# The turn from the in- to the out-projection of the convolution layer: gate tiles taken piece by piece, one weight buffer fewer, four tiles normalised

## The chip, the cores and the metric

One core of one Trainium2 chip runs the whole program. The metric is device time in microseconds (us) of one execution; before the change it was 1757.4 us, the median of three (1753.49 to 1759.08). The engines are PE (TensorE, the matmuls), DVE (VectorE), ACT (ScalarE), POOL (GpSimd) and SP (SyncE, which here only issues DMAs, in the order in which they stand in its queue).

## The reference

Two layers on 2064 tokens (16 meta tokens and 2048 of the input), 1024 channels. The change lies inside the first layer, between its first and its last matrix product:

```python
def conformer_mixer(h, w_in, b_in, w_dw, b_dw, norm_g, norm_b, w_out, b_out):
    u = h @ w_in + b_in                                  # 1024 -> 3072
    a, ga, z = jnp.split(u, 3, axis=-1)
    glu = a * jax.nn.sigmoid(ga)
    c = causal depthwise convolution of glu, 31 taps, + b_dw
    c = jax.nn.silu(layer_norm(c, norm_g, norm_b))
    return (c * jax.nn.silu(z)) @ w_out + b_out          # 1024 -> 1024
...
h = layer_norm(sqrt(2) * h + y, post_ln_g[0], post_ln_b[0])
```

The second layer is a gated linear attention on the same stream; its code is not touched.

## The kernel before, in words

**Numbers.** Each float32 operand of a large product is split into a high and a low part (`split`: ACT copies the high part, L73; DVE or POOL subtracts it, L74). A product is three matmuls for each of 8 blocks of 128 rows: high by high (L106), high by low (L107), low by high (L108). So one result tile takes 24 matmuls.

**Phase 1, the in-projection.** The tokens lie in five pieces of 414 or 412 (`XCS`), and the output channels in tiles of 128: g, a and z, eight of each. g and a make the gated value, whose 31 taps run on ACT and POOL (products and sums) and on DVE (L204). A z tile goes through silu on ACT (L258) and out to DRAM (`sz_d`), and the convolved channels to `c_d`. Weights of a tile are loaded one tile ahead (`load_w`) into one of two pairs of buffers (`pair`). The last two z tiles, 6 and 7, are special: each does piece 0 first; then `right.close()` gives memory back and `hook()` opens phase 2 (`head`, in `body`); then z6 does its other four pieces, then z7 its own.

**Phase 2, the out-projection, tile by tile of 128 tokens (17 tiles, the last of 16).** `norm(i)` loads the convolved channels of tile i into one of `CB` = 4 buffers c (L316), sums over channels (DVE L321 for even i, a tree of three POOL additions for odd i, L341 to L343), gets the mean by a small matmul (L323), subtracts it (DVE L324), squares (ACT L325), adds up (POOL tree), and by two more small matmuls (L330, L335) has the scale in PSUM, by which DVE multiplies (L336). `gate(i)` applies silu (ACT L351, 8 instructions), multiplies by z (DVE L354, the z from `szb`, L349) and splits into h_gt and l_gt (ACT L73, DVE L74). `out_proj(i)` does two halves of 24 matmuls, pj_y, adds the residual (DVE L377) and the bias (POOL L423), and normalises: L385 to L388, ACT L396, DVE L397, POOL L398, then the store to `h1_d`.

**The weights of the out-projection** come in 8 blocks of 128 rows (`load_out_w`, L364): the raw block lands in one of the two `raw` buffers (blocks 0 and 1) or in a buffer of `wrp` (`wr`; blocks 2 to 7), of which there are `WRB` = 3. ACT makes woh of it, and POOL (blocks 0, 3, 6) or DVE (the rest) makes wol. A raw buffer is free when wol has been made.

**What sets the order.** The program is recorded in the order of the Python code, with every wait on a tile that is still in use, and a scheduler then sets the order of the instructions on each engine. On the chip each engine runs its list in that order: an instruction that waits holds up those behind it. c_i+4 takes the buffer of c_i, which is free after l_gt_i.

Of the kernel before, what the change touches and what calls it, by code (L numbers as in the profile page):

```python
# [12 lines left out]
F32R = mybir.dt.float32r  # L13
# [6 lines left out]
P = 128  # L20
D = 1024
KD = D // P
# [4 lines left out]
NXC = len(XCS)  # L27
# [5 lines left out]
ZSPL = 2  # L33
# [6 lines left out]
GRATE = 2.35  # L40
VCOST = 0.53
CB = 4
WRB = 3
WMAX = 1088
SUBS = [(P * i, P) for i in range(16)] + [(2048, 16)]
BLOCKS = ((0, 528), (528, 512), (1040, 512), (1552, 512))
# [3 lines left out]
class Trunk:  # L50
# [64 lines left out]
    def phase1(self, x_cm, w1, pp, c_d, sz_d, hook):  # L115
# [22 lines left out]
        x = {}  # L138
# [26 lines left out]
        def load_w(i):  # L165
            return self.load([w1[i]], f"w{i}", nc.gpsimd)
# [46 lines left out]
        def weave(na=22 / 15, nd=20 / 15, nd1=None):  # L213
            debt[0] += na
            while debt[0] >= 1:
                debt[0] -= 1
                if act_q:
                    act_q.popleft()()
            for s in range(2):
                debt[1 + s] += nd1 if s and nd1 is not None else nd  # L220
            while max(debt[1:]) >= 1:
                for s in range(2):
                    if debt[1 + s] >= 1:
                        debt[1 + s] -= 1
                        if dve_q[s] and dve_q[s][0][0]["done"]:
                            dve_q[s].popleft()[1]()
# [3 lines left out]
        def do_g(j, w, cs=range(NXC)):  # L230
            if 0 in cs:
                glus[j] = gup[j % 3].tile([P, HIST + T], F32, tag="glu", name=f"glu{j}")
                nc.any.memset(glus[j][:, 0:HIST], 0.0)
            for c in cs:
                pg = proj(w, c, f"g{j}")
                t0, n = XCS[c]
                nc.scalar.activation(
                    glus[j][:, HIST + t0 : HIST + t0 + n], pg, AF.Sigmoid, bias=b_in[:, 8 + j : 9 + j]
                )
                weave()  # L240

        def do_a(j, w, cs=range(NXC)):
            glu = glus[j]
            for c in cs:
                pa = proj(w, c, f"a{j}")
                t0, n = XCS[c]
                dst = glu[:, HIST + t0 : HIST + t0 + n]
                nc.vector.scalar_tensor_tensor(dst, pa, b_in[:, j : j + 1], dst, op0=ALU.add, op1=ALU.mult)
                weave()
                if c in (2, NXC - 1):  # L250
                    conv_ops(j, c // 3, glu)

        def do_z(j, w, cs=range(NXC)):
            for c in cs:
# [4 lines left out]
                nc.sync.dma_start(sz_d[:, j, t0 : t0 + n], sz)  # L259
                weave()  # L260

        for c in range(NXC):
            do_g(0, w0["g"], [c])
            do_a(0, w0["a"], [c])
        order = []
# [5 lines left out]

        split = len(order) + ZSPL
        order += [(do_z, j, 16 + j, [0]) for j in range(KD - ZSPL, KD)]
        order += [(do_z, j, 16 + j, range(1, NXC)) for j in range(KD - ZSPL, KD)]
        nxt = load_w(order[0][2])
        for i, (f, j, _, *cs) in enumerate(order):
            w, nxt = nxt, load_w(order[i + 1][2]) if i + 1 < len(order) else None
# [12 lines left out]
    def phase2_open(self, pp, c_d, sz_d):  # L290
# [5 lines left out]
        self.st2w = ExitStack()  # L296
        self.wrp = self.pool(self.st2w, name="p2r", bufs=WRB, side="right")
        self.prm2 = self.lp.tile([P, 16], F32, name="prm2", bufs=1)
# [46 lines left out]
    def gate(self, i, c):  # L345
        nc = self.nc
        t0, n = SUBS[i]
        sz = self.lp.tile([P, KD, P], F32, tag="szb", name=f"szb{i}")[:, :, :n]
        nc.sync.dma_start(sz, self.sz_d[:, :, t0 : t0 + n])  # L349
        for j in range(KD):  # L350
            nc.scalar.activation(  # L351
                c[:, j], c[:, j], AF.Silu, bias=self.prm2[:, 8 + j : 9 + j], scale=self.prm2[:, j : j + 1]
            )
        nc.vector.tensor_tensor(c, c, sz, op=ALU.mult)  # L354
        h, l = (t[:, :D].rearrange("p (k n) -> p k n", n=P)[:, :, :n] for t in self.pair(f"gt{i}"))
        self.split(c, h, l, nc.vector)
        return i, h, l

# [522 lines left out]
def body(tc, x_cm, x_tok, w1, pp1, wo1, pp2, rows, w2, wv0, wv, wa2, pp3, wo2, out):  # L881
    with ExitStack() as ctx:
        dram = ctx.enter_context(tc.tile_pool(name="dram", bufs=1, space=DRAM))
        c_d = dram.tile([P, KD, T], F32, name="c_d")
        sz_d = dram.tile([P, KD, T], F32, name="sz_d")
        h1_d = dram.tile([T, D], F32, name="h1_d")
        og_d = dram.tile([P, KD, T - NMETA], F32, name="og_d")
        t = Trunk(tc, ctx)
        t.h1_d = h1_d

        def head():
            t.phase2_open(pp2, c_d, sz_d)
            for _ in range(CB - 1):
                t.norm_next()
            t.gate_next()

        t.phase1(x_cm, w1, pp1, c_d, sz_d, head)
        t.phase2(x_tok, wo1, rows[0:3], h1_d, partial(t.phase3_open, (w2, wv0, wv)))
        t.phase3_init(wa2, pp3, og_d)
        t.phase4(wo2, rows[3:5], out)  # L900
# [52 lines left out]
```

## Time and profile before

| | us |
|---|---|
| time, median of 3 (lowest, highest) | 1757.4 (1753.49, 1759.08) |
| the profiled execution | 1755.36 |
| its span, first to last instruction | 1753.6 |
| PE busy in the span | 1702.3 (97%) |
| DVE, POOL, ACT busy | 1402.4 (80%), 944.3 (54%), 842.9 (48%) |
| last z matmul to the end of the out-projection | about 555 to 785 |

The span is PE's: of the 1753.6 us some 51 are not covered by a matmul, spread over many short waits. A time in a row is counted from the span's start. In a timeline the number behind the start is the duration, xN says that N instructions are merged, and [n <-X] says that the engine was idle for n us before and what ended that. PE's rows overlap, since matmuls are pipelined: what counts is the distance from start to start.

### The profile page before, as it was taken

The numbers are of one execution on the slowest core, as the hardware profiler recorded it, in microseconds if no ns is written. First come the engines' busy times: TensorE is split into PE (matmuls) and PEld (weight loads), VectorE is DVE, ScalarE is ACT, GpSimd is POOL, SyncE is SP. The second block draws the span as 40 slices with busy tenths as digits, with TensorE's granted clock in tenths as the row PEclk, the third lists the DMA queues.
The fourth block names the chain that finished last, engine by engine and source line by source line (L and its number), as shares of the span: only waits on it lengthen the run. The fifth ranks groups of instructions, "written<-read, shape, count | busy, mean of one in ns | idle before, by whom it ended". The sixth has DMA issues, their size and how long they took to land.

```text
span 1753.6 us, 29029 instructions
## 1 busy us (share of the span) xinstructions
PE 1702.3 (97%) x11715; PEld 1514.2 (86%) x11715; DVE 1402.4 (80%) x1869; ACT 842.9 (48%) x1269; POOL 944.3 (54%) x675
## 2 busy tenths in 40 slices
PE   8999999999998998999999999999999999999998
PEld 8999999999998776767888888888888878888886
DVE  5789999999998898777666687777878687887665
ACT  6445555655544454445455455555555455541000
POOL 0879999999975788756233233333333153331000
PEclk9999999999999999999999999999999999999999
DMA  7111111111256544433113222232223322354441
GB/s 244 37 37 37 37 69 40 73 56 54 75 169 217 173 162 139 140 124 99 67 61 109 87 92 78 84 105 79 85 85 96 111 73 85 123 165 162 147 135 62
DMA packets 103910, 178.72 MB, mean 102 GB/s; under 512 B 8624, under 2 KB 68400, under 8 KB 103776
## 3 DMA queue, kind: packets, MB, share of 16 engines
q1 hardware_dynamic: 103776, 176.86, 30.0%
q8 instruction: 92, 1.51, 0.4%
q14 instruction: 42, 0.34, 0.1%
HBM read 134.70 MB, written 42.14 MB: 101 GB/s over the span
## 4 chain that ended last, share of the span: by engine, by line
PE 72%; DVE 14%; POOL 5%; ACT 4%; issue 3%; DMA 2%; SPq 0%; DVEq 0%; POOLq 0%; ACTq 0%
PE pj_y L108 4%; PE pj_y L107 4%; PE pj_y L106 4%; PE pj_g L107 3%; PE pj_g L108 3%; PE pj_g L106 3%; PE pj_z L107 3%; PE pj_a L107 3%; PE pj_z L106 3%; PE pj_a L106 3%; PE pj_z L108 3%; PE pj_a L108 3%; PE sm L755 2%; DVE A L721 1%; DVE A L720 1%
## 5 line engine op out<-in xcount | busy, mean ns | idle before, releaser
L196 POOL TENSOR_TENSOR gacc<-gacc,prod 128x1024 f32<-128x1024 f32 (+1 forms) x156 | 385.9, 2477 | 65.2 <-ACT prod L195 56.2
L204 DVE SCALAR_TENSOR_TENSOR cacc<-glu,prm,cacc 128x1024 f32<-128x1024 f32 (+1 forms) x292 | 374.9, 1294 | 7.0
L717 POOL TENSOR_TENSOR A<-b 128x256 f32<-128x256 f32 x96 | 83.2, 867 | 292.1 <-DVE b L643 110.0
L195 ACT ACTIVATE prod<-glu,prm 128x1024 f32<-128x1024 f32 (+1 forms) x156 | 179.2, 1155 | 111.0 <-POOL gacc L196 110.8
L106 PE MATMUL pj_g<-xh,h_w 128*128 128x412 f32 (+1 forms) x320 | 114.2, 357 | 6.0 <-ACT h_w L73 4.2
L107 PE MATMUL pj_g<-xl,h_w 128*128 128x412 f32 (+1 forms) x320 | 114.0, 356 | 0.3 <-DVE xl L74 0.3
L108 PE MATMUL pj_y<-woh,l_gt 128*128 128x512 f32 (+1 forms) x272 | 108.3, 403 | 5.8 <-DVE l_gt L74 5.7
L108 PE MATMUL pj_g<-xh,l_w 128*128 128x412 f32 (+1 forms) x320 | 113.0, 354 | 0.0
L107 PE MATMUL pj_a<-xl,h_w 128*128 128x412 f32 (+1 forms) x320 | 112.4, 351 | 0.0
L106 PE MATMUL pj_a<-xh,h_w 128*128 128x412 f32 (+1 forms) x320 | 112.3, 351 | 0.0
L107 PE MATMUL pj_z<-xl,h_w 128*128 128x412 f32 (+1 forms) x320 | 112.3, 351 | 0.0
L106 PE MATMUL pj_z<-xh,h_w 128*128 128x412 f32 (+1 forms) x320 | 112.2, 351 | 0.0
L108 PE MATMUL pj_z<-xh,l_w 128*128 128x412 f32 (+1 forms) x320 | 112.0, 351 | 0.0
L108 PE MATMUL pj_a<-xh,l_w 128*128 128x412 f32 (+1 forms) x320 | 111.9, 350 | 0.0
L106 PE MATMUL pj_y<-woh,h_gt 128*128 128x512 f32 (+1 forms) x272 | 110.0, 407 | 1.3 <-ACT h_gt L73 1.2
L107 PE MATMUL pj_y<-wol,h_gt 128*128 128x512 f32 (+1 forms) x272 | 109.6, 403 | 0.0
L106 PE MATMUL pj_y<-w4h,h_g 128*128 128x512 f32 x256 | 99.6, 390 | 0.0
L108 PE MATMUL pj_y<-w4h,l_g 128*128 128x512 f32 x256 | 99.6, 390 | 0.0
L107 PE MATMUL pj_y<-w4l,h_g 128*128 128x512 f32 x256 | 99.6, 390 | 0.0
L654 ACT ACTIVATE A<-A 128x512 f32<-128x512 f32 (+1 forms) x112 | 66.7, 596 | 57.7 <-POOL A L718 56.4
L388 POOL TENSOR_TENSOR rs<-rs,mhalf 128x1 f32<-128x1 f32 x16 | 14.5, 905 | 145.8 <-DVE rs L387 145.8
L377 DVE SCALAR_TENSOR_TENSOR xt<-xt,pj_y 128x512 f32<-128x512 f32 (+1 forms) x66 | 44.5, 678 | 59.5 <-PE pj_y L108 59.4
(428 smaller groups left out, 5366.5 us busy)
## 6 DMA issues: line engine op xcount, KB each, us to landing
r_w<-w SPq DMA_DIRECT2D x24, 512.0 KB, 3.3
c<-c_d SPq DMA_DIRECT2D x16, 512.0 KB, 4.5
szb<-sz_d SPq DMA_DIRECT2D x16, 512.0 KB, 4.6
xt<-x_tok SPq DMA_DIRECT2D x16, 512.0 KB, 4.6
h_d<-xt SPq DMA_DIRECT2D x16, 512.0 KB, 2.8
r_h1b<-h_d SPq DMA_DIRECT2D x16, 512.0 KB, 3.9
og_d<-og SPq DMA_DIRECT2D x32, 256.0 KB, 3.4
xt<-h_d SPq DMA_DIRECT2D x16, 512.0 KB, 3.5
```

Of the source, the lines that this page charges most:

```text
L106: mm(out, lhsT=lh, rhs=rh, start=(i == 0), stop=False)
L107: mm(out, lhsT=lh, rhs=rl, start=False, stop=False)
L108: mm(out, lhsT=ll, rhs=rh, start=False, stop=(i == n - 1))
L195: nc.scalar.activation(pr, src(k), AF.Copy, scale=tap(k))
L196: nc.gpsimd.tensor_tensor(st["g"], st["g"], pr, op=ALU.add)
L204: nc.vector.scalar_tensor_tensor(out, src(k), tap(k), acc, op0=ALU.mult, op1=ALU.add)
L377: self.nc.vector.scalar_tensor_tensor(xt[:m, es], xt[:m, es], ALPHA, ps, op0=ALU.mult, op1=ALU.add)
L654: ex = lambda o, i: nc.scalar.activation(o, i, AF.Exp, scale=1.0 / TAU)
L717: nc.gpsimd.tensor_tensor(Av[:, :, 0], mid, bv[:, :, 0], op=ALU.subtract)
L720: nc.vector.tensor_tensor(Av[:, :, 0], Av[:, :, 0], kv[:, :, 0], op=ALU.mult)
L721: nc.vector.tensor_tensor(Av[:, :, 1], Av[:, :, 1], qv[:, :, 1], op=ALU.mult)
L755: nc.tensor.matmul(sm[s : s + 32, c, 48 + 32 * i : 80 + 32 * i], lhsT=lv[m][:, w], rhs=lv[m][:, w], start=True, stop=True, skip_group_chec ...
```

## The change

Four edits. The other pieces of z6 and z7 are no longer done tile after tile but piece by piece: piece 1 of z6, piece 1 of z7, piece 2 of z6, and so on (`do_zs`), so both weight tiles stay in use to the end. The gate of tile 0 has two buffers of its own (`gt0h`, `gt0l`), since neither of the two shared pairs is free then. The raw buffers of the out-projection's weights go from three to two (`WRB`). At the opening of phase 2 four tiles are normalised instead of three.

```diff
--- before.py
+++ after.py
@@ -40,7 +40,7 @@
 GRATE = 2.35
 VCOST = 0.53
 CB = 4
-WRB = 3
+WRB = 2
 WMAX = 1088
 SUBS = [(P * i, P) for i in range(16)] + [(2048, 16)]
 BLOCKS = ((0, 528), (528, 512), (1040, 512), (1552, 512))
@@ -259,6 +259,12 @@
                 nc.sync.dma_start(sz_d[:, j, t0 : t0 + n], sz)
                 weave()
 
+        def do_zs(js, w, cs):
+            ws = [w] + [load_w(16 + j) for j in js[1:]]
+            for c in cs:
+                for j, wj in zip(js, ws):
+                    do_z(j, wj, [c])
+
         for c in range(NXC):
             do_g(0, w0["g"], [c])
             do_a(0, w0["a"], [c])
@@ -271,7 +277,8 @@
 
         split = len(order) + ZSPL
         order += [(do_z, j, 16 + j, [0]) for j in range(KD - ZSPL, KD)]
-        order += [(do_z, j, 16 + j, range(1, NXC)) for j in range(KD - ZSPL, KD)]
+
+        order.append((do_zs, range(KD - ZSPL, KD), 16 + KD - ZSPL, range(1, NXC)))
         nxt = load_w(order[0][2])
         for i, (f, j, _, *cs) in enumerate(order):
             w, nxt = nxt, load_w(order[i + 1][2]) if i + 1 < len(order) else None
@@ -352,7 +359,9 @@
                 c[:, j], c[:, j], AF.Silu, bias=self.prm2[:, 8 + j : 9 + j], scale=self.prm2[:, j : j + 1]
             )
         nc.vector.tensor_tensor(c, c, sz, op=ALU.mult)
-        h, l = (t[:, :D].rearrange("p (k n) -> p k n", n=P)[:, :, :n] for t in self.pair(f"gt{i}"))
+
+        own = [self.lp.tile([P, D], F32R, name=f"gt0{x}", bufs=1) for x in "hl"] if i == 0 else self.pair(f"gt{i}")
+        h, l = (t[:, :D].rearrange("p (k n) -> p k n", n=P)[:, :, :n] for t in own)
         self.split(c, h, l, nc.vector)
         return i, h, l
 
@@ -890,7 +899,7 @@
 
         def head():
             t.phase2_open(pp2, c_d, sz_d)
-            for _ in range(CB - 1):
+            for _ in range(CB):
                 t.norm_next()
             t.gate_next()
 
```

The scheduler makes a new order of it from the piece after the turn up to the first blocks of the second layer; before and behind that the engines' lists are the same.

On PE, where the first two tiles of the out-projection (y0 with both halves, y1 with its first) stand beside each other; woh and wol are the weights' parts, the number behind them the block, gt the gated tile. Before, the rows that reach block 4:

```order
L107 MATMUL pj_y0_0_4687<-wol3_4614,h_gt0_4310 128x512
L108 MATMUL pj_y0_0_4687<-woh3_4613,l_gt0_4311 128x512
L106 MATMUL pj_y0_0_4687<-woh4_4619,h_gt0_4310 128x512
L107 MATMUL pj_y0_1_4713<-wol3_4614,h_gt0_4310 128x512
L108 MATMUL pj_y0_1_4713<-woh3_4613,l_gt0_4311 128x512
L106 MATMUL pj_y0_1_4713<-woh4_4619,h_gt0_4310 128x512
L107 MATMUL pj_y0_0_4687<-wol4_4620,h_gt0_4310 128x512
L108 MATMUL pj_y0_0_4687<-woh4_4619,l_gt0_4311 128x512
L107 MATMUL pj_y0_1_4713<-wol4_4620,h_gt0_4310 128x512
L108 MATMUL pj_y0_1_4713<-woh4_4619,l_gt0_4311 128x512
```

And with the change:

```order
L106 MATMUL pj_y1_0_4811<-woh3_4635,h_gt1_4701 128x512
L107 MATMUL pj_y1_0_4811<-wol3_4636,h_gt1_4701 128x512
L108 MATMUL pj_y1_0_4811<-woh3_4635,l_gt1_4702 128x512
L337 MATMUL rb3_4306<-mean_80,sq3_4295 128x1
L106 MATMUL pj_y0_0_4707<-woh4_4641,gt0h_4326 128x512
L106 MATMUL pj_y0_1_4733<-woh4_4641,gt0h_4326 128x512
L106 MATMUL pj_y1_0_4811<-woh4_4641,h_gt1_4701 128x512
L107 MATMUL pj_y0_0_4707<-wol4_4642,gt0h_4326 128x512
L108 MATMUL pj_y0_0_4707<-woh4_4641,gt0l_4327 128x512
L106 MATMUL pj_y0_0_4707<-woh5_4647,gt0h_4326 128x512
```

Before, block 4 of y0 stands ahead of all of y1. Now y1's first four blocks stand ahead of it, and behind block 4 the blocks 5 to 7 come for three results at a time.

On SP, the queue of loads from the second layer's first weight (r_b0v) on; wor are the raw weights, c and szb the convolved channels and z of a tile. Before:

```order
L97 DMA r_b0v0_0_6203<-wv0 128x1088
L364 DMA wor5_4623<-wo1 128x1024
L364 DMA wor6_4629<-wo1 128x1024
L364 DMA wor7_4635<-wo1 128x1024
L349 DMA szb3_4876<-sz_d_58 128x8x128
L316 DMA c5_4854<-c_d_57 128x8x128
L349 DMA szb4_4978<-sz_d_58 128x8x128
L316 DMA c6_4958<-c_d_57 128x8x128
```

And with the change:

```order
L97 DMA r_b0v0_0_6203<-wv0 128x1088
L373 DMA wor4_4639<-wo1 128x1024
L373 DMA wor5_4645<-wo1 128x1024
L356 DMA szb3_4896<-sz_d_58 128x8x128
L323 DMA c5_4772<-c_d_57 128x8x128
L356 DMA szb4_5000<-sz_d_58 128x8x128
L373 DMA wor6_4651<-wo1 128x1024
L373 DMA wor7_4657<-wo1 128x1024
L323 DMA c6_4876<-c_d_57 128x8x128
```

Before, three blocks are loaded in a row, 5 to 7; now four are still to come at this place, two of them ahead of tile 5's channels and two behind tile 4's z.

On DVE, from the second weight block on; rb is the scale in PSUM and dg what it is made from. Before:

```order
L74 TENSOR_TENSOR wol2_4608<-wor2_4605,woh2_4607 128x1024
L334 TENSOR_SCALAR dg2_4295<-ident_73,rsl2_4291 128x128
L324 TENSOR_TENSOR c4_4752<-c4_4752,mean4_4756 128x1024
L74 TENSOR_TENSOR wol4_4620<-wor4_4617,woh4_4619 128x1024
L354 TENSOR_TENSOR c1_4257<-c1_4257,szb1_4670 128x1024
L336 TENSOR_TENSOR c2_4279<-c2_4279,rb2_4290 128x1024
L74 TENSOR_TENSOR l_gt1_4682<-c1_4257,h_gt1_4681 128x1024
L354 TENSOR_TENSOR c2_4279<-c2_4279,szb2_4772 128x1024
L74 TENSOR_TENSOR wol5_4626<-wor5_4623,woh5_4625 128x1024
```

And with the change:

```order
L74 TENSOR_TENSOR wol2_4630<-wor2_4627,woh2_4629 128x1024
L341 TENSOR_SCALAR dg2_4289<-ident_73,rsl2_4285 128x128
L331 TENSOR_TENSOR c4_4670<-c4_4670,mean4_4674 128x1024
L361 TENSOR_TENSOR c1_4251<-c1_4251,szb1_4690 128x1024
L343 TENSOR_TENSOR c2_4273<-c2_4273,rb2_4284 128x1024
L74 TENSOR_TENSOR l_gt1_4702<-c1_4251,h_gt1_4701 128x1024
L361 TENSOR_TENSOR c2_4273<-c2_4273,szb2_4794 128x1024
L338 TENSOR_SCALAR rsl3_4307<-rb3_4306 128x1
L74 TENSOR_TENSOR wol4_4642<-wor4_4639,woh4_4641 128x1024
L74 TENSOR_TENSOR wol5_4648<-wor5_4645,woh5_4647 128x1024
```

wol4 has moved from ahead of tile 1's gate to behind tile 2's.

## Rows read from the trace of the kernel before

**Rows 1.** Windows by stage (columns in the first line), all engines.

```profile
core 0: us, PE busy (x) PEld busy (x) DVE busy (x) ACT busy (x) POOL busy (x), PEclk, DMA share, GB/s
500.00:555.00 55.00, 55.00 (x299) 54.63 (x298) 46.85 (x38) 20.61 (x30) 31.15 (x25) 1.00 0.60 188
555.00:590.00 35.00, 29.46 (x126) 22.71 (x125) 30.20 (x30) 23.55 (x42) 22.67 (x17) 0.95 0.68 231
...
620.00:700.00 80.00, 70.37 (x302) 54.11 (x301) 69.82 (x86) 39.09 (x65) 68.09 (x53) 0.98 0.48 151
700.00:755.00 55.00, 53.96 (x238) 42.25 (x237) 44.74 (x62) 25.10 (x46) 41.87 (x32) 1.00 0.42 127
```

**Rows 2.** Timeline of PE, 555 to 584: start, duration, instruction, idle before.

```profile
557.46 0.71 PE L106 MATMUL pj_y<-woh,h_gt 128*128 128x512 f32 x2
...
561.85 0.79 PE L323 MATMUL mean<-sq,mean 128*128 128x128 f32 x2 [3.68 <-DVE sq L321]
...
563.30 0.63 PE L106 MATMUL pj_y<-woh,h_gt 128*128 128x512 f32 x1
...
564.95 0.39 PE L107 MATMUL pj_y<-wol,h_gt 128*128 128x512 f32 x1
...
572.14 0.50 PE L108 MATMUL pj_y<-woh,l_gt 128*128 128x512 f32 x1 [0.55 <-DVE l_gt L74]
...
582.38 0.61 PE L335 MATMUL rb<-dg,mean 128*128 128x128 f32 x4
```

**Rows 3.** Timeline of DVE, 553 to 573.

```profile
554.47 1.21 DVE L74 TENSOR_TENSOR l_gt<-c,h_gt 128x1024 fp32r<-128x1024 f32 x1
...
559.86 1.94 DVE L321 TENSOR_REDUCE sq<-c 128x128 f32<-128x1024 f32 x1 [1.56 <-DMA c<-c_d]
...
561.72 1.86 DVE L74 TENSOR_TENSOR wol<-r_wo,woh 128x1024 fp32r<-128x1024 f32 x1
...
567.39 2.31 DVE L354 TENSOR_TENSOR c<-c,szb 128x1024 f32<-128x1024 f32 x1
...
570.83 1.25 DVE L74 TENSOR_TENSOR l_gt<-c,h_gt 128x1024 fp32r<-128x1024 f32 x1
```

**Rows 4.** Timeline of POOL, 557 to 582.

```profile
560.12 2.37 POOL L74 TENSOR_TENSOR wol<-wor,woh 128x1024 fp32r<-128x1024 f32 x1
...
567.21 1.41 POOL L341 TENSOR_TENSOR sq<-sq 128x512 f32<-128x512 f32 x1 [0.82 <-ACT sq L325]
...
576.04 2.68 POOL L74 TENSOR_TENSOR wol<-wor,woh 128x1024 fp32r<-128x1024 f32 x1 [3.23 <-ACT woh L73]
```

**Rows 5.** Timeline of ACT, 557 to 576.

```profile
560.89 3.17 ACT L351 ACTIVATE c<-c,prm 128x128 f32<-128x128 f32 x8
...
569.74 1.06 ACT L73 ACTIVATE h_gt<-c 128x1024 fp32r<-128x1024 f32 x1 [2.60 <-DVE c L354]
...
573.97 2.94 ACT L73 ACTIVATE woh<-wor 128x1024 fp32r<-128x1024 f32 x3
```

**Rows 6.** DMA issues, 555 to 582: count, KB each, median us to landing.

```profile
wor<-wo SPq DMA_DIRECT2D x3, 512.0 KB, 8.4
```

**Rows 7.** DMA issues of the page, same columns, whole execution.

```profile
r_w<-w SPq DMA_DIRECT2D x24, 512.0 KB, 3.3
```

**Rows 8.** Waits of PE, 590 to 760: total, times, longest.

```profile
PE pj_y L108 <- DVE l_gt L74: 5.2, 5, 2.5
...
PE mean L323 <- DVE rsa L386: 1.2, 1, 1.2
```

**Rows 9.** Windows around one later pause of PE.

```profile
675.00:680.00 5.00, 3.08 (x12) 1.54 (x10) 5.00 (x7) 2.12 (x2) 2.60 (x3) 1.00 0.89 265
680.00:685.00 5.00, 4.59 (x14) 3.58 (x14) 4.98 (x7) 1.61 (x2) 4.92 (x5) 0.66 0.51 157
```

**Rows 10.** Groups of DVE, 590 to 700: busy, mean ns, idle before.

```profile
L397 DVE TENSOR_TENSOR xt<-xt,row 128x1024 f32<-128x1024 f32 x9 | 16.7, 1852 | 0.6 <-ACT xt L396 0.6
```

## The prediction

> **What bounds the kernel now.** I read the page first: PE is busy for 1702.3 of 1753.6 us, so only what PE waits for can be gained. The windows by stage say where that is [rows 1]. Up to 555 PE has no gap (55.00 of 55). In the turn, 555 to 590, it loses 5.5 of 35 us. From 620 to 700 it loses 9.6 and from 700 to 755 1.0; there DVE is busy for 69.8 and POOL for 68.1 of 80, and PE waits mostly for the gates, l_gt, and for small matmuls of the norms [rows 8]. PE's timeline of the turn shows one large wait: the mean of tile 4 starts at 561.85 after 3.68 us idle, since DVE summed tile 4 late, since its channels landed late [rows 2, 3]. The load of tile 4 takes tile 0's buffer, which l_gt0 frees at 554.47 + 1.21 = 555.7 [rows 3], and landing took the rest. Behind that wait matmuls last 0.63 instead of 0.39 us for a while [rows 2]: PE was at its lower clock after the pause.
>
> **The change part by part.** Times are on the clock of the profiled execution.
>
> *Pieces of z6 and z7.* The same 192 matmuls, at 55.00 us for 299 [rows 1], 0.184 each. They end at the same time, 555.5: cost nothing. The second weight tile is wanted 24 matmuls after the first; should it be late, PE would wait in a stage that has no gap now; from its load of 3.3 us [rows 7] I bound that by 0 and 3, and take 0, since both tiles already serve piece 0 in turn before the change.
>
> *Tile 0's gate.* The small matmuls of tiles 1 and 2 now stand 7 to 8 z matmuls earlier, 8 x 0.184 = 1.5 us. I let l_gt0, tile 4's load and its sum move by that: mean 4 at 560.3 instead of 561.85. Little of it reaches the products. The seventh matmul behind mean 4 needs wol1 on DVE, and that waits for POOL's wol3: DVE's row started at 561.72 and took 1.86, that is 1.09 from the end of POOL's (560.12 + 2.37 = 562.49) [rows 3, 4]. POOL's wol3 does not move, so wol1 is ready at 563.6 as before, and the matmul starts there instead of at 564.95 [rows 2]: -1.3, between 0 and -3.1 (564.95 less 561.85, if all waits of that stretch went).
>
> *Tile 1's gate.* wol4 no longer stands ahead of it on DVE. The product with z moves from 567.39 to 566.0, ahead of POOL's addition of 567.21, and so takes about 1.2 instead of 2.31 [rows 3, 4]. h_gt1 (1.06, now starting at 569.74 [rows 5]) ends at 568.2, l_gt1 behind POOL's addition at 569.7. y1's first low-by-high matmul moves from 572.14 [rows 2] to 569.8. Ten more of its matmuls at 70.37 / 302 = 0.233 [rows 1] bring PE to 572.1.
>
> *One raw buffer fewer.* This is what costs. wor4 now waits for wol2, at 564.7, where the queue is full: the three blocks issued from there took 8.4 us [rows 6], 573.1. One load fewer stands ahead of it, so I take 571.6. ACT has finished tile 2's silu by then (568.4 + 3.17 [rows 5] = 571.5), woh4 takes 2.94 / 3 = 0.98 [rows 5], and PE waits until 572.6. wol4 now stands behind tile 2's gate on DVE: 574.0. PE does blocks 4 and 5 of three results and is at mean 5 at 577.5; tile 5's load, issued behind l_gt1 into the same backlog, lands at about 576, with POOL's tree 578.6. wor6 waits for wol4, 574.0, and lands between 577.3 (3.3 us [rows 7]) and 582.4 (8.4 [rows 6]); I take 578.8, nearer to the free one, since the backlog is almost through. woh6 is then ready at 579.8, and wol6, which is POOL's at 2.37 (the wol3 row [rows 4]), at 582.2; the same wol6 ended at 576.04 + 2.68 = 578.7 before. Fifteen matmuls remain with block 7: both results of y0 and the first of y1 are done at 586.0 instead of 582.4 [rows 2]. So the turn costs +3.6, gains of tiles 0 and 1 already in it. With wor6 at the early end mean 5 decides and it is +2.6; at the late end +7.3. New pauses of PE could bring the low clock again: 675 to 680, with 3.08 of 5 us busy, was followed by a window at 0.66 in which 14 matmuls took 4.59 us, 1.3 more than at 0.233 [rows 9]. I take 0 for it and keep 1.3.
>
> *Four tiles normalised.* This does little: c4's load waits for l_gt0 in both programs, and c3's stands in the same place of SP's queue. The second effect of the new order counts more: mean 5 and 6 now stand some 40 and 80 rows earlier on PE, and the norms of tiles 7 to 12 about 40 rows earlier than before, so a gate is asked for later after its norm.
>
> *What comes back later.* From 620 to 755 PE waits for 10.6 us [rows 1], and 80 us at 0.98 cost 1.6. PE that comes 3.6 later while DVE and POOL do not finds 3.6 of this gone. For the deeper norms I add 1.4, half of what is left of the waits for l_gt (5.2 less 3.6 is 1.6, and the 1.2 of a mean [rows 8]). So -5.0, between 0 and -12.2.
>
> **Sum.** +3.6 - 5.0 = -1.4. The profiled execution took 1755.36 (span 1753.6 and 1.8 around it), so 1754.0; the median of the runs is 2.0 above the profiled one, so I predict 1756.0. About 5.3 us, 0.3%, is what a measurement of this kernel can tell from no change.
>
> **A rule weighed.** L397 on DVE takes 1852 ns on the mean from 590 to 700 [rows 10], where an instruction of the same size took 1.21 alone [rows 3], and the wol1 row above ends 1.09 after POOL's. The Trainium skill ("SBUF — State Buffer", section "Who interferes with whom") says that a DVE instruction with two inputs in SBUF and a GpSimd instruction that reads SBUF exclude each other: the second one stands still until the first is through. The trace agrees at these rows. By that rule the exclusive work of a tile is the same in either order, and the out-projection would end when it did before: the sum would be 0 instead of -1.4.
>
> **Rivals.** *Fixed work of DVE and POOL.* No instruction is added or removed, and between 620 and 700 both are busy for over 85% [rows 1]. If their work, waits for each other included, sets the end of the stage, neither the late weights nor the deeper norms show: 1757.4. Against it: from 700 to 755 POOL is busy for 41.9 of 55 only. *Slower: the late weights are not made up.* The second half of y1 and all that follows start 3.6 to 7.3 later; since y0's evacuations start the additions of POOL and the L397 of DVE, these are late too, and the norms queue behind them on engines that have no room. Then nothing comes back: +7.3 from wor6 at its late end, no clock: 1764.7. It decides from the point where wor6 lands after about 580. For it: 8.4 us for the three blocks [rows 6]. *Faster: the norms' lead.* If rb of tiles 7 to 12, 40 rows earlier (9 us), takes away the waits of 620 to 755 altogether with the low clock there, +3.6 - 12.2 = -8.6: 1748.8. For it: the longest wait is 2.5 us for an l_gt [rows 8], which such a lead covers; against it, that a mean or a scale asked for earlier may itself be what PE waits for. *The edit does not do what it says.* In ACT's list woh0 stays behind the last silu of z in both programs, so laying the weights over pieces that end early starts nothing earlier; this is already in the sum.
>
> **Chances.** Forecast as summed 0.30; fixed work 0.18; not made up 0.24; norms' lead 0.28. The first two lie within 0.3%. So faster 0.28, same 0.48, slower 0.24. The range goes to both outer cases and a little beyond, for the bounds of wor6 and the clock: 1747 to 1767.
>
> **What would show it.** Right: z ends at the same time; mean 4 about 1.5 us earlier and wol1 not; the rows of block 4 and 6 on PE preceded by waits for woh and wol, and y0 complete near 586; fewer waits for l_gt from 620 on, and more for means and scales. Wrong: wor6 landing after 580, or waits for l_gt as long as before (then slower); no wait at block 6, or PE without gaps from 620 on (then faster); a gap among the z matmuls.

## The result and the profile after

| | before | after |
|---|---|---|
| time, median (lowest, highest), us | 1755.45 (1752.34, 1759.08) | 1771.22 (1770.5, 1772.16) |
| span of the profiled execution, us | 1753.6 | 1768.7 |

The change makes the kernel slower: 1.0089 times the time before, with a 95% interval of 1.0066 to 1.0112, or 15.8 us by the medians (15.6 by the ratio). The forecast was 1756.0, and its range ended at 1767.

Where the time went is seen in the windows by stage of the changed kernel, with the columns of [rows 1]:

```profile
500.00:555.00 55.00, 54.82 (x298) 54.24 (x296) 47.43 (x38) 20.07 (x31) 30.49 (x24) 1.00 0.58 178
555.00:590.00 35.00, 24.34 (x92) 18.59 (x92) 27.20 (x26) 22.46 (x39) 22.95 (x18) 0.85 0.73 253
620.00:700.00 80.00, 67.99 (x291) 52.34 (x289) 66.62 (x77) 31.58 (x51) 53.77 (x43) 0.98 0.47 148
700.00:755.00 55.00, 51.27 (x217) 40.63 (x217) 46.98 (x63) 26.23 (x45) 45.73 (x38) 0.94 0.46 142
```

Against [rows 1], PE is busy for 5.1 us less in the turn (24.34 for 29.46, with 92 instructions for 126), 2.4 less from 620 to 700 and 2.7 less from 700 to 755. From 620 to 700 DVE and POOL are busy for less as well (66.62 for 69.82, 53.77 for 68.09), from 700 to 755 for more (46.98 for 44.74, 45.73 for 41.87). Neither fills its stretch, so its busy time alone doesn't set the end. To have numbers that add up, also over stretches at the lower clock, I take for each two neighbouring matmuls the distance from start to start, less the median distance of that kind of pair's first instruction in the same kernel, and add these up. I call it PE's loss:

| PE's loss, us | before 540 | the turn, 540 to 620 | 620 to 800 | behind 800 |
|---|---|---|---|---|
| before | 6.8 | 8.8 | 19.3 | 55.8 |
| after | 5.5 | 17.4 | 27.2 | 55.7 |

So the turn costs 8.6 and the stage behind it 7.8. Ahead of 540 the loss is 1.3 smaller. The last z matmul of the changed kernel starts at 554.02, that of the kernel before at 555.27:

```profile
554.02 0.35 PE L108 MATMUL pj_z<-xh,l_w 128*128 128x412 f32 x1
```

```profile
555.27 0.35 PE L108 MATMUL pj_z<-xh,l_w 128*128 128x412 f32 x1
```

This isn't shown to be a gain of the change: in experiment 12, whose lists are those of before, that matmul starts at 554.21. So comparisons with [rows 2] below are counted from it, "behind z", that is from 554.0 and 555.3.

**The turn.** PE's timeline of the changed kernel, columns as in [rows 2]:

```profile
556.00 0.35 PE L337 MATMUL rb<-mean,sq 128*128 128x1 f32 x2 [1.18 <-ACT woh L73]
561.13 0.77 PE L330 MATMUL mean<-sq,mean 128*128 128x128 f32 x2 [4.20 <-DVE sq L328]
...
570.81 0.50 PE L108 MATMUL pj_y<-woh,l_gt 128*128 128x512 f32 x1 [1.39 <-DVE l_gt L74]
...
575.01 0.50 PE L107 MATMUL pj_y<-wol,gt0h 128*128 128x512 f32 x1 [0.54 <-DVE wol L74]
...
579.97 0.49 PE L330 MATMUL mean<-sq,mean 128*128 128x128 f32 x2 [0.98 <-POOL sq L350]
...
583.09 0.80 PE L107 MATMUL pj_y<-wol,gt0h 128*128 128x512 f32 x1 [1.37 <-POOL wol L74]
583.68 0.63 PE L108 MATMUL pj_y<-woh,gt0l 128*128 128x512 f32 x1
584.11 0.63 PE L107 MATMUL pj_y<-wol,gt0h 128*128 128x512 f32 x1
584.54 0.63 PE L108 MATMUL pj_y<-woh,gt0l 128*128 128x512 f32 x1
...
588.25 0.38 PE L342 MATMUL rb<-dg,mean 128*128 128x128 f32 x2
```

The mean of tile 4 (561.13) stands 7.1 us behind z, and stood 6.55 behind it before (561.85 less 555.3). The waits at 575.01 (block 4) and 583.09 (block 6) are what the prediction named as signs; between them stands a wait at mean 5 (579.97). The three results y0, y0 and the first of y1 end with the last row, 34.2 us behind z, for 27.1 before (582.38 [rows 2]): +7.1. DVE of the changed kernel shows why tile 4 was no earlier, and how the gates follow:

```profile
559.06 1.92 DVE L328 TENSOR_REDUCE sq<-c 128x128 f32<-128x1024 f32 x1 [2.01 <-DMA c<-c_d]
...
569.19 1.57 DVE L74 TENSOR_TENSOR l_gt<-c,h_gt 128x1024 fp32r<-128x1024 f32 x1
572.53 1.22 DVE L361 TENSOR_TENSOR c<-c,szb 128x1024 f32<-128x1024 f32 x1 [1.78 <-ACT c L358]
...
573.74 2.35 DVE L74 TENSOR_TENSOR wol<-wor,woh 128x1024 fp32r<-128x1024 f32 x2
```

The sum over tile 4 waits for its load, as before [rows 3]. Counted from z, the load was issued about half a us earlier (at 553.88 here, at 555.72 before) and landed about half a us later, since it took longer. The DMA issues (KB each, median us to landing) in the changed kernel from 553 to 554.5:

```profile
c<-c_d SPq DMA_DIRECT2D x1, 512.0 KB, 5.2
```

and in the kernel before from 555 to 556:

```profile
c<-c_d SPq DMA_DIRECT2D x1, 512.0 KB, 4.1
```

The late weight itself, wor6, landed at 579.5. ACT of the changed kernel then makes woh6:

```profile
579.53 1.06 ACT L73 ACTIVATE woh<-wor 128x1024 fp32r<-128x1024 f32 x1 [4.19 <-DMA wor<-wo]
```

and its POOL wol6:

```profile
580.67 2.37 POOL L74 TENSOR_TENSOR wol<-wor,woh 128x1024 fp32r<-128x1024 f32 x1 [0.75 <-ACT woh L73]
```

And PE goes to its lower level (1.2 GHz) twice in the turn, each time behind a wait. Windows of the changed kernel:

```profile
555.00:560.00 5.00, 0.93 (x4) 0.52 (x4) 2.99 (x4) 5.00 (x9) 3.96 (x3) 0.87 0.82 253
560.00:565.00 5.00, 3.87 (x10) 3.23 (x11) 5.00 (x5) 2.82 (x6) 2.94 (x2) 0.50 1.03 417
...
580.00:585.00 5.00, 3.44 (x12) 2.65 (x13) 3.69 (x5) 5.00 (x11) 2.88 (x2) 0.76 0.34 99
```

**The stage behind it.** What PE waits for from 590 to 760 in the changed kernel (columns as in [rows 8]):

```profile
PE mean L330 <- DVE sq L328: 5.8, 4, 3.0
PE rb L342 <- DVE rsa L396: 3.8, 2, 2.6
PE mean L330 <- POOL sq L350: 2.6, 2, 2.3
PE rb L337 <- POOL sq L350: 2.0, 2, 1.1
PE rb L342 <- DVE dg L341: 1.6, 1, 1.6
```

The waits for l_gt, 5.2 us in [rows 8], are gone, as the prediction had it. Others stand in their place, for means and scales, and these five groups add up to 15.8 us. (That this is also the difference of the medians is chance.) Before, all groups of the same view added up to 10.6, so the waits grew by 5.2. Most of the rest of the 7.8 is by estimate the clock: from 700 to 755 it was 0.94, where it had been 1.00 [rows 1], and 0.06 of 55 are 3.3 us.

### The profile page after: what moved, and what is told of

It reads as the page before. It is cut to its first block, busy times and chain, and to the rows that moved or that the text cites. A ratio compares the mean times of both kernels' runs of the same rounds, so it can differ in the third digit from the quotient of the medians.

```text
span 1768.7 us, 29046 instructions
## 1 busy us (share of the span) xinstructions
PE 1704.5 (96%) x11715; PEld 1516.0 (86%) x11715; DVE 1408.3 (80%) x1869; ACT 841.9 (48%) x1269; POOL 936.6 (53%) x675
## 4 chain that ended last, share of the span: by engine, by line
PE 40%; DVE 11%; ACT 4%; POOL 4%; issue 2%; DMA 1%; DVEq 0%; POOLq 0%; ACTq 0%
PE pj_y L108 3%; PE pj_y L106 3%; PE pj_y L107 3%; PE sm L764 1%; DVE A L730 1%; DVE A L729 1%; PE att L736 1%; PE pj_b3v L106 1%; POOL xt L432 1%; PE pj_b3v L107 1%; PE pj_b3v L108 1%; PE pj_b2v L106 1%; PE oT L798 1%; PE pj_b2v L108 1%; PE pj_b2v L107 1%
## 5 line engine op out<-in xcount | busy, mean ns | idle before, releaser
L108 PE MATMUL pj_y<-woh,l_gt 128*128 128x512 f32 (+1 forms) x256 | 103.5, 404 | 1.4 <-DVE l_gt L74 1.4
L106 PE MATMUL pj_y<-woh,h_gt 128*128 128x512 f32 (+1 forms) x256 | 104.4, 408 | 0.2 <-DVE xt L386 0.2
L107 PE MATMUL pj_y<-wol,h_gt 128*128 128x512 f32 (+1 forms) x256 | 103.8, 405 | 0.0
```

The source lines that it names most:

```text
L106: mm(out, lhsT=lh, rhs=rh, start=(i == 0), stop=False)
L107: mm(out, lhsT=lh, rhs=rl, start=False, stop=False)
L108: mm(out, lhsT=ll, rhs=rh, start=False, stop=(i == n - 1))
```

## The experiments

All are compared with the kernel before on the same chip; a ratio stands with its 95% interval, times in us are medians, and a difference in us is the ratio's, of 1755.5 (that of the medians is up to 1 us away). The first eight weigh five theories of the cost. A: two separate costs, late weights at the turn and norms that stand earlier on PE behind it. B: the late weights alone, whose loss is never made up and grows. C: the order by pieces. D: a norm wants the buffer of a tile whose gate has just ended. E: what costs is the order that the scheduler makes on PE, whatever edit leads to it.

**1. Late weights alone** (on the kernel before)

```diff
-WRB = 3
+WRB = 2
```

> The kernel before with only the raw buffers of the weights reduced from three to two (WRB = 2). After minus before is 15.8 us; in the profiles the first three half tiles (y0, y0, y1) end 5.9 us later (7.1 less a start 1.2 earlier), and the rest arises behind. Theory A (two separate costs: late weights about +7 at the turn, and norms placed earlier on PE about +9 later): this has the first alone, 1755.5 + 7 = about 1762.5, with y1's first half ending near 589 and the waits behind it as before. Theory B (the late weights alone, never made up and growing): about 1771. Theory C (the piecewise z is what costs): 1755.5.

Measured 1765.34, ratio 1.0061 (1.0045 to 1.0077), +10.7, nearer to A's 1762.5 than to B's 1771. In the profile PE's loss is 19.2 in the turn and 21.4 from 620 to 800: 10.4 more in the turn, 2.1 more behind it. The profiled execution took 1772.31, the longest of the six and 7 us above their median, so this split isn't that of the +10.7; but the shortest of the six, 1762.1, is above all of the kernel before too. The loss isn't made up. PE's timeline of this run:

```profile
564.34 0.80 PE L323 MATMUL mean<-sq,mean 128*128 128x128 f32 x2 [6.11 <-DVE sq L321]
...
584.75 1.31 PE L106 MATMUL pj_y<-woh,h_gt 128*128 128x512 f32 x3 [2.03 <-ACT woh L73]
587.19 0.79 PE L107 MATMUL pj_y<-wol,h_gt 128*128 128x512 f32 x1 [1.14 <-POOL wol L74]
```

Beside the two waits for block 6 there is the wait for mean 4, which stands 9.0 us behind z (555.3).

**2. Four tiles alone** (on the kernel before)

```diff
-            for _ in range(CB - 1):
+            for _ in range(CB):
```

> The kernel before with only one more tile normalised at the opening of phase 2 (four for three). Theory A: the turn as before (y1's first half ends near 582), the later waits for means and scales in place of those for l_gt: about 1755.5 + 9 = 1764. Theory B: 1755.5, since no weight comes later. Theory C: 1755.5. Its norms stand partly earlier, partly later on PE than in the changed kernel, so theory A allows 1759 to 1766.

Measured 1777.07, 1.0124 (1.011 to 1.0139), +21.8: more than the whole change, and beyond every forecast (A's ended at 1766). The turn loses 1.7 more than before, the stage behind it 18.1 more (37.4). PE's waits from 620 to 800:

```profile
PE pj_y L106 <- ACT h_gt L73: 10.8, 3, 9.1
PE rb L335 <- DVE dg L334: 6.7, 2, 5.9
```

The longest is at the first product of tile 7. PE's timeline there, from the second scale matmul of tile 7 on:

```profile
648.99 0.39 PE L335 MATMUL rb<-dg,mean 128*128 128x128 f32 x2
...
663.15 0.80 PE L106 MATMUL pj_y<-woh,h_gt 128*128 128x512 f32 x1 [9.14 <-ACT h_gt L73]
663.74 0.63 PE L107 MATMUL pj_y<-wol,h_gt 128*128 128x512 f32 x1
```

DVE's, where the sum of a later tile and the statistics of an earlier one stand ahead of the scaling of tile 7 (L336):

```profile
647.39 2.03 DVE L321 TENSOR_REDUCE sq<-c 128x128 f32<-128x1024 f32 x1 [0.32 <-DMA c<-c_d]
649.32 1.28 DVE L385 BATCH_NORM_STATS2 sta<-xt 128x6 f32<-128x512 f32 x2
...
651.61 1.21 DVE L336 TENSOR_TENSOR c<-c,rb 128x1024 f32<-128x1024 f32 x1
```

and ACT's:

```profile
652.86 0.88 ACT L351 ACTIVATE c<-c,prm 128x128 f32<-128x128 f32 x2 [10.18 <-DVE c L336]
...
662.05 1.04 ACT L73 ACTIVATE h_gt<-c 128x1024 fp32r<-128x1024 f32 x1
```

From the scaling of tile 7 on DVE (651.61) to its h_gt (663.09) 11.5 us pass: eight silu, between them work for other tiles, the product with z, the split. PE had little in its list to fill them. How much, the list tells: the number of PE's rows between the second scale matmul of a tile (L335) and its first product. I call it the lead; for tiles 7 to 15 of this kernel it is 21, 11, 41, 89, 22, 25, 102, 151, 75, and before it is 54, 55, 52, 35, 52, 66, 66, 49, 50. At 0.233 us a row [rows 1], 21 rows are 4.9 us.

**3. The changed kernel with three tiles**

```diff
-            for _ in range(CB):
+            for _ in range(CB - 1):
```

> The changed kernel with three tiles normalised at the opening instead of four (piecewise z, own gate buffers and two raw buffers kept). Theory A: the turn's cost stays, the later one goes: about 1762 with the first half of y1 ending near 588. Theory B: 1771, as the changed kernel. Theory C: 1771 as well; set against the run with two raw buffers alone, it shows what the pieces cost.

Measured 1767.47, 1.0064 (1.0052 to 1.0077), +11.2. It lies between A's 1762 and the 1771 of B and C. Turn 16.7, behind it 21.9, in an execution of 1768.53, near the median: 7.9 and 2.6 more than before. The time is that of experiment 1, so pieces and gate buffer add nothing that shows here.

**4. The changed kernel with three raw buffers** (the room comes from one of z's buffers; no run takes that alone)

```diff
-WRB = 2
+WRB = 3
...
-        szp = self.pool(self.st2, name="p1z", bufs=3, side="right")
+        szp = self.pool(self.st2, name="p1z", bufs=2, side="right")
```

> The changed kernel with three raw buffers again; the space comes from the buffers of silu(z), two instead of three. Theory A: the turn is no later than before or up to 2 us earlier (y1's first half ends at 580 to 582), the later waits stay: 1755.5 + 9 - 1 = about 1763. Theory B: 1754 to 1756. Theory C: still near 1771. Should two buffers for silu(z) hold PE up, gaps show among the z matmuls, up to 3 us.

Measured 1775.47, 1.0111 (1.0098 to 1.0124), +19.5. All forecasts missed it (A had 1763, B 1754 to 1756, C 1771). In the turn PE no longer waits for block 6 (1.4 and 0.2 us in the changed kernel), only 1.2 us for DVE's wol; the turn still loses about 6 more than before, and the kernel is slower than the changed one. Its leads for tiles 7 to 15 are 22, 25, 100, 149, 48, 96, 22, 25, 106: short ones again.

**5. and 6. A fifth buffer for c, with three and with four tiles** (on the kernel before)

```diff
-CB = 4
+CB = 5
...
-            for _ in range(CB - 1):
+            for _ in range(3):
```

(5; number 6 has `range(CB - 1)`, which is four.)

> The kernel before with five buffers for the convolved channels instead of four, still three tiles normalised at the opening. Tile 4's load then waits for no gate. Theory D (each norm wants the buffer of a tile whose gate has just ended, so loads come late; the fifth buffer takes that away): the 3.7 us wait for tile 4's mean goes, about 1751. Theory E (what counts is the order on PE that the scheduler makes, not when a buffer comes free): 1755 to 1760, with another wait in its place.

> The kernel before with five buffers and four tiles normalised at the opening: the relation of the three buffers' worth of slack is that of the kernel before again, one tile further on. The run with four tiles and four buffers was at 1777, 21.5 us over before. Theory D: that cost goes, 1751 to 1757. Theory E: four tiles at the opening cost what they did, 1765 to 1777.

Measured 1762.35, 1.0035 (1.0024 to 1.0047), +6.1, and 1773.9, 1.0099 (1.0084 to 1.0113), +17.4. Both of D's forecasts fail; the first is also above E's 1760, the second is in E's range. With the fifth buffer four tiles still cost 11.3 more than three, for 21.8 with four buffers. Lists and buffer both differ there, so what part of the difference the buffer has isn't told apart. The shortest lead of number 6 is 7 rows, at tile 11.

**7. A fourth raw buffer** (on the kernel before)

```diff
-WRB = 3
+WRB = 4
```

> The kernel before with four raw buffers of the weights instead of three; two cost 10 us. Late weights as the cause: block 5 is there before the turn as well, and the first half of y1 ends no later than before; since the trace of before shows no wait for a weight, 1753 to 1756. Should the number of buffers work by the order that the scheduler makes rather than by the weights' arrival, it may be off by 5 to 10 in either direction.

Measured 1763.27, 1.0043 (1.0028 to 1.0057), +7.5: above the 1753 to 1756 foretold if late weights are the cause, and within the 5 to 10 left to a new order. The profiled execution, 1769.27, is the longest of eight and 6 us above their median; in it PE loses 3.0 more in the turn and 6.2 more from 620 to 800, so these aren't parts of the 7.5. More room for the weights, and slower. So the turn of the kernel before isn't short of raw buffers; that the new order is what costs is argued, by exclusion.

**8. Pieces and gate buffer alone** (the changed kernel with both other edits undone)

```diff
-WRB = 2
+WRB = 3
...
-            for _ in range(CB):
+            for _ in range(CB - 1):
...
-        szp = self.pool(self.st2, name="p1z", bufs=3, side="right")
+        szp = self.pool(self.st2, name="p1z", bufs=2, side="right")
```

> The piecewise z and the own gate buffers alone: three raw buffers, three tiles normalised; two buffers of silu(z) instead of three make the space. Theories A and B: no cost, 1753 to 1757, with the end of z where it was. Theory C: slower by several us. With four tiles normalised the same kernel was at 1775.5, so this also shows what the fourth tile costs: about 20 by theory A.

Measured 1764.17, 1.0049 (1.0035 to 1.0062), +8.6: 5.4 in the turn, 2.4 behind it. A and B had no cost. Alone the pieces cost something; beside the late weights (3) they don't. The costs don't add up.

The next four set E against another theory, L: that a deeper lead of the norms costs by itself.

**9. Late weights and four tiles, no pieces** (on the kernel before, both edits of 1 and 2)

> The kernel before with two raw buffers and four tiles normalised at the opening; the last two z tiles stay whole and tile 0's gate stays in the shared pair. What is left to the changed kernel is the order by pieces and the gate buffer. If the pieces cost nothing, the time is the changed kernel's, 1771 (1768 to 1774). If the costs of the two parts add, 1755.6 + 10.7 + 21.7 = 1788, and the pieces give back 17. If only the order that the scheduler makes counts (theory E), neither sum need hold: this order has the second scale matmul of tile 7 about 112 rows ahead of y7, as the changed kernel has (121), and not 48 as with four tiles alone, so its time should be that of the late weights and a rest, 1766 to 1775, without the wait of 9 us ahead of y7.

Measured 1769.45, 1.0081 (1.0068 to 1.0095), +14.2. Not the sum of 1 and 2 (32.5), but nearly the changed kernel, as foretold if the pieces cost nothing. The leads of tiles 7 to 15 are 54 to 108: no short one.

**10. Four tiles at the opening, none beside the first product**

```diff
-            for _ in range(CB - 1):
+            for _ in range(CB):
...
-            self.norm_next()
+            if i:
+                self.norm_next()
```

> The kernel before with four tiles normalised at the opening, but no tile normalised beside the first product: from tile 4 on the norms stand as far ahead of the products as before. Theory L (the deeper lead itself costs, since a norm then wants the buffer of a tile whose gate has just been made): the cost of four tiles, 21.7, goes, 1753 to 1759. Theory E (what counts is the order on PE that comes out; each order other than the one of before has cost 6 to 20): 1760 to 1770, though every buffer and every norm from tile 4 on is as before.

Measured 1759.85, 1.0023 (1.0013 to 1.0034), +4.0: between the two forecasts. From 620 to 800 PE loses 19.3, as before. Leads 50 to 54 for tiles 4 to 15. So the fourth tile by itself costs little; 18 us of experiment 2 come with the lists that follow from it, tile by tile. By this run alone they could come with the deeper lead, too; but experiment 9 has the same depth as 2, and over experiment 1 it costs 3.5 us, not 21.8.

**11. Two tiles at the opening**

```diff
-            for _ in range(CB - 1):
+            for _ in range(CB - 2):
```

> The kernel before with two tiles normalised at the opening instead of three, so the lead is one shorter to the end. Theory L: a shorter lead holds fewer buffers; gates are asked for nearer to their norm, so some waits for l_gt come, 1753 to 1762. Theory E: 1761 to 1776, by waits of PE for means and scales at other places than before.

Measured 1785.05, 1.0168 (1.0153 to 1.0183), +29.5. A shorter lead of the norms is the slowest of all, so L's forecast (1753 to 1762) falls; E's (1761 to 1776) is 9 us low. Leads for tiles 6 to 14: 14, 17, 101, 98, 8, 49, 51, 5, 9. PE's list has the first and the second scale matmul of tile 8 next to each other, with DVE, POOL and DVE again between them. PE's timeline of this run:

```profile
646.24 0.28 PE L330 MATMUL rb<-mean,sq 128*128 128x1 f32 x2
652.11 0.80 PE L335 MATMUL rb<-dg,mean 128*128 128x128 f32 x2 [5.59 <-DVE dg L334]
```

**12. Gate ahead of norm in the loop**

```diff
-            self.norm_next()
             self.gate_next()
+            self.norm_next()
```

> The kernel before with gate_next ahead of norm_next in the loop over the tiles: the same instructions, the same buffers in the same numbers, another order of recording. Theory L: nothing that it names changes, 1753 to 1759. Theory E: the scheduler places the small matmuls elsewhere only where the recorded order decides; if its order on PE differs in the rows from 620 to 755, 1760 to 1770, and if it is nearly that of before, as it is up to tile 10, 1753 to 1759. It tells little between the two unless it is slower.

Measured 1755.09, 1.0003 (0.9994 to 1.0011). All five lists come out as before but for the numbers in names, so it tells nothing between the theories; it shows how closely two measurements of one program agree. Its last z matmul:

```profile
554.21 0.35 PE L108 MATMUL pj_z<-xh,l_w 128*128 128x412 f32 x1
```

The last four take load off DVE and POOL, to see what it has to do with what is not made up. They leave out the bias of the out-projection and the gain and bias of the normalisation behind it, so they no longer compute the layer. Each is the kernel before, experiment 1, experiment 2 or the changed kernel, with

```diff
-        nc.vector.tensor_tensor(r[:n], r[:n], g[:n], op=ALU.mult)
-        nc.gpsimd.tensor_tensor(r[:n], r[:n], b[:n], op=ALU.add)
...
-            nc.gpsimd.tensor_tensor(xt[:m], xt[:m], b_out[:m], op=ALU.add)
```

**13. to 16. Before, late weights, four tiles and the change, with less load**

> The kernel before without the bias of the out-projection (POOL, L423) and without the gain and bias of the normalisation behind it (DVE L397, POOL L398), which are left out of the result: 17 instructions less on DVE and 34 less on POOL, which took 23.8 and 68.3 us from 590 to 755. It is the measure for the three that follow. PE lost 19.3 us from 620 to 800 against its own pace; if it loses that because DVE and POOL are full, most of it goes: 1738 to 1746. If the order of the lists decides whatever the load, 1750 to 1756.

> The same work left out, and two raw buffers instead of three. With the work in, this alone cost 10.7, of which PE lost 10.4 in the turn (540 to 620). If the load of DVE and POOL is what keeps the turn's loss from being made up, it is made up only as far as the stage still has waits, which the lighter stage hasn't: 8 to 11 over l_before, all of it in the turn. If it can be made up at all, under 5.

> The same work left out, and four tiles normalised at the opening. With the work in, this alone cost 21.7, of which 18 from 620 to 800. Theory of the load (the deeper lead costs because DVE and POOL are full, and then what a product needs next stands behind work for later tiles): the loss goes, 0 to 4 over l_before. Theory of the order (whatever the load, the small matmuls of the norms stand at wrong places of PE's list): 12 to 25 over l_before.

> The same work left out of the changed kernel. With the work in it cost 15.8: 8.6 in the turn and 7.8 from 620 to 800. Theory of the load: only the turn's part stays, 7 to 11 over l_before. Theory of the order: 13 to 20 over l_before.

| with less load | time (lowest, highest) | over l_before | with the load | loss in the turn | 620 to 800 |
|---|---|---|---|---|---|
| l_before | 1736.66 (1735.63, 1737.07) | | | 8.9 | 3.5 |
| l_wrb2 | 1744.57 (1743.35, 1746.34) | 7.9 | 10.7 | 17.7 | 3.6 |
| l_norm4 | 1741.77 (1740.61, 1744.72) | 5.1 | 21.8 | 9.2 | 8.3 |
| l_after | 1744.08 (1743.76, 1748.3) | 7.4 | 15.6 | 16.8 | 3.5 |

The windows of l_before, then of l_after:

```profile
540.00:620.00 80.00, 74.37 (x343) 61.79 (x342) 60.37 (x74) 44.26 (x75) 38.31 (x39) 0.98 0.59 195
620.00:700.00 80.00, 80.00 (x365) 65.02 (x364) 69.01 (x95) 46.25 (x78) 42.72 (x48) 1.00 0.62 191
700.00:755.00 55.00, 55.00 (x254) 44.34 (x253) 32.29 (x58) 26.07 (x48) 11.81 (x17) 1.00 0.37 120
```

```profile
540.00:620.00 80.00, 69.59 (x309) 57.60 (x307) 58.43 (x71) 47.78 (x83) 40.05 (x39) 0.94 0.64 208
620.00:700.00 80.00, 80.00 (x365) 65.25 (x364) 63.24 (x94) 40.00 (x69) 37.41 (x44) 1.00 0.57 171
700.00:755.00 55.00, 55.00 (x249) 44.26 (x249) 32.10 (x59) 26.65 (x48) 11.34 (x18) 1.00 0.36 117
```

From 620 to 755 PE has no gap in either. What the turn lost is then all that is left (the change loses 7.9 more there, and takes 7.4 longer), and nothing can give it back, since PE itself is the bound. So the later 7.8 of the change, waits for DVE and POOL, went when load was taken away; l_after is in its forecast of 7 to 11, l_wrb2 0.1 below its own of 8 to 11, and l_before 1.3 below its 1738. But the lists were made anew as well: up to about 600 us PE's are the same, and behind that 591 places differ between before and l_before and 404 between the changed kernel and l_after. The new one has longer leads still (in the traces, where a small matmul is two rows, about 109 to 134 for tiles 7 to 15, where the changed kernel has 87 to 103), so long leads alone need not make PE wait; that the load alone took the waits away isn't shown. For four tiles alone the reading is less clean still: l_norm4 is beyond its forecast of 0 to 4, by one wait from 620 to 800,

```profile
PE rb L330 <- POOL sq L343: 3.1, 1, 3.1
```

and the lighter load changed its lists too; its leads are 59 to 142, where experiment 2 had 11 to 151. Load and order both changed there, and which of them took the 17 us away isn't told apart.

## Why the prediction was wrong

**The sum.** Foretold were +3.6 in the turn and -5.0 behind it. PE's loss says +8.6 and +7.8. (The +3.6 was counted at the end of three results, where +7.1 was measured; the losses from there to 620 are the rest.) By the prediction's own terms it is a little less: 582.2 and fifteen matmuls at 0.233 are 585.7, not 586.0, and the late end of wor6 makes +7.2, not +7.3.

**Pieces of z at no cost: right here.** There is no gap among the z matmuls (54.82 of 55), and without the pieces the change costs 14.2 for 15.6, a difference within the two intervals (1.0068 to 1.0095, 1.0066 to 1.0112). Alone they are not free (8).

**Gates of tiles 0 and 1, -1.3 and -2.4: wrong.** This step let tile 4's load and sum move with l_gt0. The issue moved by about 0.5, and the landing took 5.2 in place of 4.1. Mean 4 came 7.1 us behind z, where 5.0 was foretold (560.3 less 555.3); l_gt1 ended 16.8 behind it (569.19 + 1.57), where 14.4 was foretold. All that follows was about 2 late by that: tile 2's silu, wol4, and with it the load of wor6, which landed 25.5 behind z, not 23.5.

**One raw buffer fewer, +3.6: right mechanism, wrong size.** wor6, woh6 on ACT, wol6 on POOL and then block 7 is the chain that ended last, as worked out; wol6 ended at 29.0 behind z (580.67 + 2.37), not 26.9. The rest is the clock, which I bounded by 1.3 and took at 0: from wol6 to the end of the three results 5.2 us passed (588.25 less 583.09), for 3.8 foretold, and the rows behind 583.09 start 0.43 apart. 2.1 and 1.4 make the 3.5 between +3.6 and +7.1. The landing stands within the prediction's bounds (22.0 to 27.1 behind z), the 1.4 a tenth beyond its 1.3.

**What comes back later, -5.0 between 0 and -12.2: this is the step that failed.** It took PE's waits of 620 to 755 for slack that a later PE fills. They were not: PE's waits from 590 to 760 grew from 10.6 to 15.8 us, and the stage lost 7.8 more instead of 5.0 less. Experiment 3 carries the turn's loss through to the end of the stage with 2.6 on top (1, in its long execution, with 2.1); only the rival "not made up" had that. And the range excluded a loss: "between 0 and -12.2". The deeper norms did take the waits for l_gt away, but by standing where their own inputs were not ready: mean and rb now stop PE. The prediction listed more waits for means and scales as a sign of being right, and its signs for slower hardly came: waits for l_gt as long as before (there are none from 590 to 760), or wor6 landing after 580 (it landed at 579.5, or 25.5 behind z, which would be 580.8 in the kernel before). The rival "norms' lead" named this danger and its price was never worked out; added to the other rival's 1764.7, the 7.8 would give 1772.5.

**Four tiles normalised, "does little": wrong as argued, for a reason that I didn't look at.** c4's load does wait for l_gt0 in both programs, and n4_once, with the fourth tile and without the shift behind it, is 4.0 slower. But norms and gates are taken in turns from there on, so one more at the opening shifts every later norm by a tile, and the lists are made anew. In the changed kernel this gave long leads, 83 to 145 rows for tiles 3 to 16, so no product waited for its gate; in experiments 2, 4 and 6 it gave shortest leads of 7 to 22 rows, and cost 21.8 (2), 10.9 (4 against 8) and 11.3 (6 against 5). With two raw buffers the fourth tile costs 3.5 (9 against 1) and 4.4 (the change against 3).

**The rule weighed** (the Trainium skill, "SBUF — State Buffer", section "Who interferes with whom"). By it the exclusive work of DVE and POOL gave the same end for the out-projection in either order. Between 620 and 700 DVE and POOL are busy for 66.6 and 53.8 us now, for 69.8 and 68.1 [rows 1], and from 700 to 755 for 47.0 and 45.7, for 44.7 and 41.9. Over both stretches less of their work is done in the same time, so no fixed amount of it sets the end. As a rule on two engines it isn't touched by this; as a forecast of the stage it failed, and with it the rival "fixed work".

**What stays open.** Why the kernel before has little loss with leads of 35 to 82 rows (124 for tile 4), when experiment 7 with 45 to 96 loses 6.2 more from 620 to 800, the lead alone doesn't say: long leads trade waits for gates against waits for means. E says that the list decides, and not which list is good. Whether load or order took the later 7.8 away in l_after isn't told apart. And 5.4 us of n4_once's loss lie behind 800, scattered in pieces of 2 or 3 us over a single profile; they weren't followed.

## What to carry to other kernels

Waits of an engine are slack only if what it waits for doesn't move with it: take away the work of the engines waited for, and see whether the loss stays (here the turn's 8 stayed and the later 7.8 went, though the lists were new too). A count such as "one more tile ahead" in front of an alternating loop shifts the whole loop, so read the new lists to the end of the stage, not only at the edit, and count for each tile the rows between its last small matmul and its first product. Where a scheduler remakes the order, the costs of two edits don't add (10.7 and 21.8 made 14.2), so the parts have to be measured together as well.

## What the runs showed of the hardware

The load of tile 4, 512 KB, landed after 4.1 us and, issued half a microsecond earlier as counted from z, after 5.2, so half a microsecond later by that count. With two raw buffers alone mean 4 came still later, 9.0 us behind z. A load moved earlier need not land earlier. The granted clock was 0.50 from 560 to 565, behind a stretch with 0.93 of 5 us busy, and 0.76 from 580 to 585, behind waits of 0.98 and 1.37 us only, and matmuls there started 0.43 us apart in place of 0.233.
